# Unsplit fp32 operands in the first matmuls behind a normalisation: a two-layer decoder trunk on one core

## The chip, the cores and the metric

The kernel runs on one core of a Trainium2 chip. The metric is the device time of one execution in microseconds (us). The kernel before takes 1955.97 us, the median of three runs between 1953.8 and 1957.2.

## The reference

The reference is a decoder trunk of two layers on 256 tokens of width 1024, all in float32. Cut to what matters here:

```python
for l in range(2):
    h = rms_norm(x, norm1_g[l]) * (1.0 + sc1) + sh1
    z, xbc, dt_raw, mq, mk, mv, sq, sk, sv = split(h @ w_in[l])
    y = concat(ssd(z, xbc, dt_raw), moba(mq, mk, mv), swa(sq, sk, sv)) @ w_out[l]
    x = x + g1 * y
    h = rms_norm(x, norm2_g[l]) * (1.0 + sc2) + sh2
    q = h @ peer_wq[l]            # 8 heads x 256 columns
    # each half of q against 128 keys, top 16 of each, top 16 of the sums: 16 experts
    x = x + g2 * experts(h, chosen, peer_u[l], peer_v[l])
return rms_norm(x, final_g)
```

## The kernel before, in words

A product of two float32 matrices is made of three matmuls in the type fp32r (`mm3`, L165 to L168). Each operand is split into a high part (a cast to fp32r, on ScalarE: `wH` of weights at L159, `hH` of activations at L258) and a low part (what the cast left over: `wL` at L162, `hL` at L259), and high times high, high times low and low times high are added up in PSUM. The low part of a block of weights comes from VectorE (`low` is "v") or from GpSimd (as a whole, or as two halves where `low` is "h").

Weights come in blocks of 128 x 1024, four k-rows of 128 for 256 columns. `fetch` (L145) loads a block into one of five `raw` buffers by a DMA of the SP queue; `split` (L151) writes its parts into one of three `wH` and one of three `wL` buffers. A buffer is free for its next block when the last reader of the block in it is done. For `raw` that is the split.

`norm_rows`, `norm_scaled` and `norm_banks` make the scaled rows `xn` (L234) and transpose them on TensorE (L242). `norm_h` (L245) turns each of four transposed banks into `h32`, two k-rows of 256 tokens, one half on VectorE (L257) and one on ScalarE (L255), and then into `hH` and `hL`. There are two `norm_h` in a layer. The one ahead of the mixers goes in four steps of one bank (`FIRST`, L46): behind each step come the matmuls that need its two k-rows, for the column chunks `mq`, `mk` and `sq` in turn. The one behind the mixers does all four banks at once; behind it `peer` (L671) begins with `query(0)` (L713): 256 columns of `wq`, two blocks, `low` "h".

Most of the order on each engine is chosen by a planner that lists the instructions in advance by its own estimate of their times. Two things bind it: within `manual_schedule` (PE in `peer`, L711) the engine keeps the order of the program, and `pinned()` (L227) puts the instructions that its block issues on the engine of `pin[0]` behind `pin[0]`. `pin[0]` is the latest power operation of `norm_rows` on GpSimd (L222); so `query(0)`'s low parts on GpSimd come behind it.

Behind the eight queries and their scores (L725) come the passes over `peer_u` (L689) and `peer_v` (L899), in the same three-matmul form.

Of the kernel before, what the change touches and what calls it, by code (L numbers as in the profile page):

```python
# [13 lines left out]
F32 = mybir.dt.float32  # L14
# [3 lines left out]
ALU = mybir.AluOpType  # L18
# [4 lines left out]
P = 128  # L23
D = 1024
S = 256
NC = 2
KD = D // P
# [27 lines left out]
HB = 3  # L55
# [12 lines left out]
COLS = {"adab": 0, "n1": 48, "n2": 56, "cw": 64, "cb": 96, "mg": 104}  # L68
# [13 lines left out]
def trunk(ctx: ExitStack, tc: tile.TileContext, x_in, c_in, ada, cols, rows, w_in, w_out, wq, keysT, uT, vT, fg, out, dbg=None):  # L82
    nc = tc.nc
    V, A, G, T = nc.vector, nc.scalar, nc.gpsimd, nc.tensor
# [3 lines left out]
    st = ctx.enter_context(tc.tile_pool(name="st", bufs=2))  # L88
# [6 lines left out]
    def bank(kind=None):  # L95
        if kind is None:
            turn[0] += 1
            kind = "pa" if turn[0] % 2 else "pb" if turn[0] % 4 < 2 else "pc"
        return (ps_a if kind == "pa" else ps_b).tile([P, 512], F32, tag=kind, name=kind)
# [35 lines left out]
    hs = [None, None]  # L135
# [9 lines left out]
    def fetch(src):  # L145
        n = src.shape[-1]
        raw = st.tile([P, D + 1], F32, tag="raw", name="raw", bufs=RB)
        nc.sync.dma_start(raw[:, :n], src)
        return raw[:, :n]
# [15 lines left out]
    def mm3(o, l, r, start, stop):  # L165
        T.matmul(o, l[0], r[0], start=start, stop=False)  # L166
        T.matmul(o, l[0], r[1], start=False, stop=False)  # L167
        T.matmul(o, l[1], r[0], start=False, stop=stop)  # L168
# [44 lines left out]
    def norm_rows(pool, xt, c):  # L213
# [8 lines left out]
        pin[0] = G.tensor_tensor(out=r, in0=ms, in1=mhalf, op=ALU.pow).ins  # L222
        return r

    pin = [None]

    def pinned():  # L227

        return tc.issue_after(pin[0]) if PIN else nullcontext()
# [7 lines left out]
    def norm_banks(xn, k20=0, n=KD // 2, kind=None):  # L237
        banks = [bank(kind) for _ in range(n)]
        for c in range(NC):
            for k in range(2 * k20, 2 * (k20 + n)):  # L240
                o = k % 2 * S + c * P
                T.transpose(banks[k // 2 - k20][:, o:o + P], xn[c][:, k * P:(k + 1) * P], ident)  # L242
        return banks

    def norm_h(pool, banks, colt, modc, gcol, sh, sc, k20=0):  # L245
        k0, n = 2 * k20, 2 * len(banks)
        acol = pool.tile([P, KD], F32, tag="acol", name="acol")
        V.scalar_tensor_tensor(out=acol[:, k0:k0 + n], in0=modc[:, sc, k0:k0 + n], scalar=1.0, in1=colt[:, gcol + k0:gcol + k0 + n], op0=ALU.add, op1=ALU.mult)
        for k2 in range(k20, k20 + len(banks)):
            h32 = pool.tile([P, 2, S], F32, tag="t2k", name="h32", bufs=3)  # L250
            for q in range(2):
                k = 2 * k2 + q
                src = banks[k2 - k20][:, q * S:(q + 1) * S]
                if q and H32A:
                    A.activation(h32[:, q, :], src, AF.Identity, scale=acol[:, k:k + 1], bias=modc[:, sh, k:k + 1])  # L255
                else:
                    V.tensor_scalar(out=h32[:, q, :], in0=src, scalar1=acol[:, k:k + 1], scalar2=modc[:, sh, k:k + 1], op0=ALU.mult, op1=ALU.add)  # L257
            A.copy(hs[0][:, 2 * k2:2 * k2 + 2, :], h32)  # L258
            V.tensor_tensor(out=hs[1][:, 2 * k2:2 * k2 + 2, :], in0=h32, in1=hs[0][:, 2 * k2:2 * k2 + 2, :].bitcast(F32), op=ALU.subtract)  # L259

    def gated_add(pool, xt, c, n, acc, gb):

# [29 lines left out]
    def proj_channels(src, off, w, low=LOWM):  # L292

        pcs = [bank() for _ in range(w // P)]
        for _ in proj_parts(pcs, src, off, w, KD, low):
            pass
        return pcs

    def proj_parts(pcs, src, off, w, step, low=LOWM):

        for k0, n, h, lo in units(src, off, w, low):
            yield
            for k1 in range(0, n, step):
                for cb, pc in enumerate(pcs):
                    for kk in range(k1, min(n, k1 + step)):
                        k = k0 + kk
                        sl = slice(kk * w + cb * P, kk * w + (cb + 1) * P)
                        mm3(pc[:, :S], (h[:, sl], lo[:, sl]), (hs[0][:, k, :], hs[1][:, k, :]), k == 0, k == KD - 1)
                yield

    def proj_tokens(src, off, w, low=LOWM):
# [12 lines left out]
    def mixers(l, xp, mx, xt, xn, modc, colt, early, late):  # L324
        if True:
# [53 lines left out]
            off = {}  # L379
# [4 lines left out]
            wl = w_in[l]  # L384
# [99 lines left out]

            first = {n: [bank(b) for b in kinds] for n, kinds in (("mq", ("pa", "pa")), ("mk", ("pa", "pa")), ("sq", ("pb", "pb")))}
            part = {n: proj_parts(pcs, wl, *off[n], 2) for n, pcs in first.items()}
            for p, names in enumerate(FIRST):
                banks = norm_banks(xn, p, 1, "pc")
                pre, post = names
                pre = pre.split()  # L490
                ada = early(mx, 2 * p, 2)
                for i in range(max(len(pre), len(ada))):
                    if i < len(ada):
                        ada[i]()
                    if i < len(pre) and pre[i] != "-":
                        with pinned() if p == 1 else nullcontext():
                            next(part[pre[i]])
                norm_h(xp, banks, colt, modc, COLS["n1"], 0, 1, p)
                for n in post.split():
                    next(part[n])  # L500
            for g in part.values():
                assert next(g, None) is None
            tick[0] = later
            mq = to_sb(first["mq"], "mq")
            mk = to_sb(first["mk"], "mk")
            sq = to_sb(first["sq"], "sq")
            half = lambda t, i: t[64 * i:64 * (i + 1), :]
# [127 lines left out]
            pcs = [[bank() for _ in range(NC)] for _ in range(2)]  # L635
# [9 lines left out]
            for n in range(2):  # L645
                for q in range(2):
                    h, lo = split(fetch(w_out[l, n, 1, :, q * 1024:(q + 1) * 1024]), LOWM(q))
# [10 lines left out]
            xn = []  # L658
# [5 lines left out]
            for c in range(NC):  # L664
                for n in range(2):
                    gated_add(xp, xt, c, n, pcs[n][c], gb)
                xn.append(norm_scaled(xp, xt, c, norm_rows(xp, xt, c)))
            norm_h(xp, norm_banks(xn), colt, modc, COLS["n2"], 3, 4)


    def peer(l, steps):  # L671
# [23 lines left out]
        with tc.tile_pool(name=f"topk{l}", bufs=1, reuse_waits="tile") as tp:  # L695
# [15 lines left out]
            order.enter_context(tc.manual_schedule(engines={mybir.EngineType.PE}))  # L711

            def query(h):  # L713
                with pinned() if h == 0 else nullcontext():
                    pq = proj_channels(wq[l], h * D * 256, 256, lambda q: "h")
                q = new([P, 2, S], "q", bufs=2)
                for i in range(2):
                    A.copy(q[:, i, :], pq[i][:, :S])
                return q
# [204 lines left out]
    xp = xs.enter_context(tc.tile_pool(name="x0", bufs=1))  # L924
# [4 lines left out]
    xn = [norm_scaled(xp, xt, c, norm_rows(xp, xt, c)) for c in range(NC)]  # L929
    for l in range(DEPTH):  # L930
        ada0 = {}

        def early(pool, k0, n):
            if l:
                return []
            if not ada0:
                ada0.update({m: ada_steps(0, m, mod[0], pool) for m in range(2)})
            return [ada0[m][k] for k in range(k0, k0 + n) for m in range(2)]
# [24 lines left out]
        xp = xs.enter_context(tc.tile_pool(name=f"x{l + 1}", bufs=1, reuse_waits="tile"))  # L963
# [24 lines left out]
        else:  # L988
            xn = [norm_scaled(xp, xt, c, rs[c]) for c in range(NC)]
# [64 lines left out]
```

## Time and profile before

| | |
|---|---|
| median of three runs | 1955.97 us |
| the profiled execution | 1956.04 us, of which the span from the first to the last instruction is 1954.3 us |
| PE (TensorE) busy | 1875.9 us, 96% of the span |
| DVE (VectorE) busy | 1430.5 us, 73% |
| ACT (ScalarE) busy | 966.3 us, 49% |
| POOL (GpSimd) busy | 498.1 us, 25% |
| DMA | 376.53 MB, 193 GB/s in the mean |

The span is 1.7 us shorter than the execution's time. Times in the rows below are counted from the start of the span. The busy time of PE counts matmuls that overlap once; a matmul's own duration is longer than the distance from its start to the next one's. The granted clock is given as a share of 2.4 GHz, so 0.50 is 1.2 GHz. PEld is the weight load.

### The profile page before, as it was taken

What the parts mean: (1) busy time and instruction counts of PE and PEld (TensorE: products, weight loads), DVE (VectorE), ACT (ScalarE), POOL (GpSimd) and SP (SyncE); (2) the same over time, 40 slices, a digit from 0 to 9 for tenths busy, and PEclk for the clock granted to TensorE, in tenths of its full rate; (3) what the DMA queues carried; (4) which work ended last, traced back from release to release, by engine and by line L of the source; (5) the groups of instructions that cost most, each with busy time, mean ns of one, the idle gap of its engine ahead of it and who ended that gap; (6) DMA issues with size and microseconds to landing.
All of it is one profiled execution on the core that took longest, in us unless ns stands there. A gap on an engine that the chain in (4) does not pass through costs nothing. (4 is left out here: it accounts for less than half of the span.)

```text
span 1954.3 us, 33671 instructions
## 1 busy us (share of the span) xinstructions
PE 1875.9 (96%) x12864; PEld 1714.5 (88%) x12864; DVE 1430.5 (73%) x2679; ACT 966.3 (49%) x1502; POOL 498.1 (25%) x303
## 2 busy tenths in 40 slices
PE   4898999999999999999989989999999999999998
PEld 3786999999999888888878789999999998888886
DVE  6866799889963898966667669968899346666665
ACT  3464445444444454545547444455444445555544
POOL 5675799100024001000001167960000320000001
PEclk8898999999999999999989989999999999999999
DMA  7863455444455999866543344554444555655553
GB/s 276 288 211 116 162 182 182 167 162 153 161 166 172 380 348 350 312 199 195 192 131 123 118 143 150 186 178 159 160 155 160 173 193 190 223 196 193 193 194 116
DMA packets 103557, 376.53 MB, mean 193 GB/s; under 512 B 12002, under 2 KB 12258, under 8 KB 102756
## 3 DMA queue, kind: packets, MB, share of 16 engines
q1 hardware_dynamic: 103396, 374.39, 56.3%
q8 instruction: 100, 1.64, 0.3%
q14 instruction: 61, 0.50, 0.1%
HBM read 371.20 MB, written 3.15 MB: 192 GB/s over the span
## 5 line engine op out<-in xcount | busy, mean ns | idle before, releaser
L159 ACT CAST wH<-raw 128x1024 fp32r<-128x1024 f32 (+1 forms) x602 | 629.3, 1046 | 530.7 <-PE pu L167 349.9
L162 DVE TENSOR_TENSOR wL<-raw,wH 128x1024 fp32r<-128x1024 f32 x437 | 535.3, 1226 | 223.6 <-ACT wH L159 222.8
L162 POOL TENSOR_TENSOR wL<-raw,wH 128x512 fp32r<-128x512 f32 (+2 forms) x224 | 438.4, 1977 | 595.7 <-ACT wH L159 586.0
L166 PE MATMUL pu<-hH,wH 128*128 128x256 f32 x2048 | 581.2, 284 | 3.9 <-ACT act L693 3.9
L168 PE MATMUL pu<-hH,wL 128*128 128x256 f32 x2048 | 575.7, 281 | 0.0
L167 PE MATMUL pu<-hL,wH 128*128 128x256 f32 x2048 | 575.4, 281 | 0.0
L167 PE MATMUL pacc<-wL,aH 128*128 128x512 f32 x1024 | 399.2, 390 | 0.0
L168 PE MATMUL pacc<-wH,aL 128*128 128x512 f32 x1024 | 398.5, 389 | 0.0
L166 PEld LDWEIGHTS pu<-hH,wH 128*128 128x128 f32 x2048 | 386.9, 189 | 4.6 <-ACT act L693 4.6
L167 PEld LDWEIGHTS pu<-hL,wH 128*128 128x128 f32 x2048 | 387.1, 189 | 0.0
L168 PEld LDWEIGHTS pu<-hH,wL 128*128 128x128 f32 x2048 | 386.5, 189 | 0.0
L166 PE MATMUL pacc<-wH,aH 128*128 128x512 f32 x1024 | 277.4, 389 | 0.0
L892 ACT CAST aH<-act 128x256 fp32r<-128x256 f32 x256 | 104.0, 408 | 340.3 <-PE pacc L167 339.0
L167 PEld LDWEIGHTS pacc<-wL,aH 128*128 128x128 f32 x1024 | 192.2, 188 | 40.4 <-DVE wL L162 0.8
L168 PEld LDWEIGHTS pacc<-wH,aL 128*128 128x128 f32 x1024 | 192.2, 188 | 39.7
L166 PEld LDWEIGHTS pacc<-wH,aH 128*128 128x128 f32 x1024 | 192.1, 188 | 39.8
L893 DVE TENSOR_TENSOR aL<-act,aH 128x256 fp32r<-128x256 f32 x256 | 108.4, 425 | 108.6 <-ACT aH L892 108.2
L980 POOL TENSOR_TENSOR x<-x,fgb 128x512 f32<-128x512 f32 x2 | 3.4, 1700 | 352.4 <-ACT junk L218 352.4
L166 PE MATMUL pa<-hH,wH 128*128 128x256 f32 x256 | 75.7, 308 | 12.5 <-ACT hH L258 8.7
L167 PE MATMUL pa<-hL,wH 128*128 128x256 f32 x256 | 76.4, 301 | 1.9 <-DVE hL L259 1.8
L168 PE MATMUL pa<-hH,wL 128*128 128x256 f32 x256 | 75.6, 299 | 0.9 <-POOL wL L162 0.9
L854 DVE SCALAR_TENSOR_TENSOR act<-pc,act 128x160 f32<-128x160 f32 (+30 forms) x126 | 38.5, 306 | 44.5 <-PE pc L848 44.3
(428 smaller groups left out, 2470.9 us busy)
## 6 DMA issues: line engine op xcount, KB each, us to landing
raw<-in_uT_dram SPq DMA_DIRECT2D x256, 512.0 KB, 3.6
raw<-in_vT_dram SPq DMA_DIRECT2D x256, 512.0 KB, 4.4
adaw<-in_ada_dram SPq DMA_DIRECT2D x56, 512.5 KB, 5.9
raw<-in_ada_dram SPq DMA_DIRECT2D x40, 512.5 KB, 4.9
raw<-in_w_in_dram SPq DMA_DIRECT2D x38, 512.0 KB, 4.8
raw<-in_wq_dram SPq DMA_DIRECT2D x32, 512.0 KB, 3.6
raw<-in_w_out_dram SPq DMA_DIRECT2D x16, 512.0 KB, 3.9
raw<-in_w_in_dram SPq DMA_DIRECT2D x8, 392.0 KB, 3.5
```

The source lines that it names most:

```text
L159: A.copy(h[:, :n], src)
L162: eng.tensor_tensor(out=lo[:, o:o + step], in0=src[:, o:o + step], in1=h[:, o:o + step].bitcast(F32), op=ALU.subtract)
L166: T.matmul(o, l[0], r[0], start=start, stop=False)
L167: T.matmul(o, l[0], r[1], start=False, stop=False)
L168: T.matmul(o, l[1], r[0], start=False, stop=stop)
L854: V.scalar_tensor_tensor(out=a, in0=pv[:, lo:hi, :], scalar=1.0 / WSCALE, in1=a, op0=ALU.mult, op1=ALU.mult)
L892: A.copy(aH, act)
L893: V.tensor_tensor(out=aL, in0=act, in1=aH.bitcast(F32), op=ALU.subtract)
L980: (V if c else G).tensor_tensor(out=xt[:, c, cs], in0=xt[:, c, cs], in1=fgb[:, cs], op=ALU.mult)
```

## The change

For layer 1's chunk `mq`, and for `query(0)` of both layers, the three matmuls on split operands become one matmul on the float32 operands as they are: `raw` as loaded and `h32` as computed, in the new `proj_parts_whole`. These blocks are not split. `h32` is kept: where `norm_h` does all four banks, it stands in two buffers of the ring `wL` (four k-rows in each); where it does one bank, in the ring `t2k` as before. The making of `hH` and `hL` is put into functions that are called behind the matmuls on `h32` instead of ahead of them. `pin[0]` becomes the last `h32` instruction on VectorE in the `norm_h` of four banks; `query(0)` is no longer pinned, `query(1)` is, and its low parts move from GpSimd to VectorE. Layer 0's first `norm_h` and its chunks stay as they are.

```diff
-    def norm_h(pool, banks, colt, modc, gcol, sh, sc, k20=0):
+    def norm_h(pool, banks, colt, modc, gcol, sh, sc, k20=0, whole=None):
...
+        halves = []
         for k2 in range(k20, k20 + len(banks)):
-            h32 = pool.tile([P, 2, S], F32, tag="t2k", name="h32", bufs=3)
+            if whole is None or k20 or len(banks) == 1:
+                h32 = pool.tile([P, 2, S], F32, tag="t2k", name="h32", bufs=3)
+            elif k2 % 2 == 0:
+                four = st.tile([P, 1024], F32, tag="wL", name="h32", bufs=HB).rearrange("p (k t) -> p k t", k=4)
+                h32 = four[:, 0:2, :]
+            else:
+                h32 = four[:, 2:4, :]
+            if whole is not None:
+                whole.append(h32)
...
+                    d = V.tensor_scalar(out=h32[:, q, :], in0=src, scalar1=acol[:, k:k + 1], scalar2=modc[:, sh, k:k + 1], op0=ALU.mult, op1=ALU.add)
+                    if whole is not None and len(banks) > 1:
+                        pin[0] = d.ins
+
+            def half(k2=k2, h32=h32):
+                A.copy(hs[0][:, 2 * k2:2 * k2 + 2, :], h32)
+                V.tensor_tensor(out=hs[1][:, 2 * k2:2 * k2 + 2, :], in0=h32, in1=hs[0][:, 2 * k2:2 * k2 + 2, :].bitcast(F32), op=ALU.subtract)
+            if whole is None:
+                half()
+            else:
+                halves.append(half)
+        return halves
...
+    def proj_parts_whole(pcs, src, off, w, step, hw):
+
+        ku = 1024 // w
+        blk = src[off:off + KD * P * w].rearrange("(r p q f) -> r p q f", p=P, r=KD // min(KD, 2 * ku), f=ku * w)
+        for k0 in range(0, KD, ku):
+            raw = fetch(blk[k0 // (2 * ku), :, k0 // ku % 2, :])
+            yield
+            for k1 in range(0, ku, step):
+                for cb, pc in enumerate(pcs):
+                    for kk in range(k1, k1 + step):
+                        k = k0 + kk
+                        T.matmul(pc[:, :S], raw[:, kk * w + cb * P:kk * w + (cb + 1) * P], hw[k // 2][:, k % 2, :], start=k == 0, stop=k == KD - 1)
                 yield
...
+            whole = None
+            if l:
+                whole = []
+                part["mq"] = proj_parts_whole(first["mq"], wl, *off["mq"], 2, whole)
...
-                norm_h(xp, banks, colt, modc, COLS["n1"], 0, 1, p)
+                halves = norm_h(xp, banks, colt, modc, COLS["n1"], 0, 1, p, whole)
                 for n in post.split():
                     next(part[n])
+                    if n == "mq":
+                        for f in halves:
+                            f()
...
-            norm_h(xp, norm_banks(xn), colt, modc, COLS["n2"], 3, 4)
+            whole2[:] = []
+            whole2_halves[:] = norm_h(xp, norm_banks(xn), colt, modc, COLS["n2"], 3, 4, 0, whole2)
...
             def query(h):
-                with pinned() if h == 0 else nullcontext():
-                    pq = proj_channels(wq[l], h * D * 256, 256, lambda q: "h")
+                if h == 0:
+
+                    pq = [bank() for _ in range(2)]
+                    for _ in proj_parts_whole(pq, wq[l], 0, 256, 4, whole2):
+                        pass
+                    for f in whole2_halves:
+                        f()
+                else:
+                    with pinned() if h == 1 else nullcontext():
+                        pq = proj_channels(wq[l], h * D * 256, 256, lambda q: "v" if h == 1 else "h")
```

## Rows read from the trace of the kernel before

**Rows 1.** The table of stretches: the stretch and its length, then busy time and number of instructions of PE, PEld, DVE, ACT and POOL, the granted clock, the DMA engines' mean busy share and GB/s.

```profile
175.00:200.00 25.00, 19.39 (x116) 17.02 (x114) 13.09 (x19) 11.88 (x23) 16.01 (x13) 0.80 0.38 133
200.00:300.00 100.00, 100.00 (x855) 100.00 (x854) 91.75 (x408) 49.04 (x65) 85.04 (x45) 1.00 0.52 174
...
600.00:1010.00 410.00, 403.67 (x1962) 341.08 (x1961) 296.58 (x407) 204.23 (x299) 24.61 (x22) 0.99 0.73 259
...
1130.00:1160.00 30.00, 25.35 (x177) 23.73 (x177) 15.20 (x46) 12.95 (x22) 22.58 (x18) 0.83 0.46 160
```

**Rows 2.** The timeline of all engines at the end of layer 0's mixers: start, duration (of the whole group where it is x2 or more), engine, line, operation, out<-in, and the idle time ahead of it with what ended it.

```profile
179.22 0.89 DVE L234 TENSOR_SCALAR xn<-x,hr 128x512 f32<-128x512 f32 x2 [0.44 <-POOL hr L222]
...
179.76 0.44 PE L242 MATMUL pa<-ident,xn 128*128 128x128 f32 x2 [2.51 <-DVE xn L234]
...
180.47 0.38 PE L242 MATMUL pc<-ident,xn 128*128 128x128 f32 x2
180.82 8.68 POOL L162 TENSOR_TENSOR wL<-raw,wH 128x512 fp32r<-128x512 f32 x6
180.89 2.88 DVE L234 TENSOR_SCALAR xn<-x,hr 128x512 f32<-128x512 f32 x2 [0.66 <-POOL hr L222]
...
182.42 0.69 PE L242 MATMUL pa<-ident,xn 128*128 128x128 f32 x2 [1.56 <-DVE xn L234]
...
183.69 0.53 DVE L257 TENSOR_SCALAR h<-pa,acol,modc 128x256 f32<-128x256 f32 x1
...
184.32 0.56 ACT L255 ACTIVATE h<-pa,modc,acol 128x256 f32<-128x256 f32 x1 [4.73 <-DVE h L257]
...
185.24 0.61 ACT L258 CAST hH<-h 128x512 fp32r<-128x512 f32 x1
...
185.88 0.79 DVE L259 TENSOR_TENSOR hL<-h,hH 128x512 fp32r<-128x512 f32 x1 [0.75 <-ACT hH L258]
...
185.90 0.58 PE L166 MATMUL pa<-hH,wH 128*128 128x256 f32 x1 [0.96 <-ACT hH L258]
...
188.41 0.58 PE L167 MATMUL pa<-hL,wH 128*128 128x256 f32 x1
```

**Rows 3.** The timeline of PE alone, on through layer 0's query 0 (its last matmul is the one ahead of 195.08) and to the scores behind query 1.

```profile
191.78 0.41 PE L167 MATMUL pb<-hL,wH 128*128 128x256 f32 x1
...
192.20 0.28 PE L166 MATMUL pa<-hH,wH 128*128 128x256 f32 x1
192.32 0.28 PE L167 MATMUL pa<-hL,wH 128*128 128x256 f32 x1
...
194.96 0.28 PE L168 MATMUL pb<-hH,wL 128*128 128x256 f32 x1
195.08 0.28 PE L166 MATMUL pa<-hH,wH 128*128 128x256 f32 x1
...
200.84 1.05 PE L725 MATMUL pa<-kt,q 128*128 128x128 f32 x8
201.65 0.36 PE L166 MATMUL pb<-hH,wH 128*128 128x256 f32 x1
```

**Rows 4.** The table of stretches again, columns as in rows 1, for short stretches around the three places where the clock falls and rises.

```profile
182.00:186.00 4.00, 2.33 (x9) 1.53 (x9) 3.25 (x6) 1.68 (x4) 4.00 (x4) 0.50 0.34 98
...
192.00:193.00 1.00, 1.00 (x9) 1.00 (x9) 0.00 (x0) 0.72 (x1) 0.00 (x0) 0.91 0.13 49
...
1144.00:1145.00 1.00, 1.00 (x8) 1.00 (x8) 0.00 (x0) 0.98 (x1) 0.00 (x0) 0.75 0.00 0
...
1004.00:1005.00 1.00, 1.00 (x8) 1.00 (x7) 0.00 (x0) 0.00 (x0) 0.00 (x0) 0.72 0.00 0
```

**Rows 5.** The timeline of all engines at the end of layer 1's mixers, columns as in rows 2; the last of them is the first matmul of query 1.

```profile
1132.64 2.88 DVE L234 TENSOR_SCALAR xn<-x,hr 128x512 f32<-128x512 f32 x2 [0.66 <-POOL hr L222]
...
1137.65 0.58 PE L166 MATMUL pa<-hH,wH 128*128 128x256 f32 x1 [0.96 <-ACT hH L258]
...
1147.03 0.28 PE L166 MATMUL pa<-hH,wH 128*128 128x256 f32 x1
```

**Rows 6.** The timeline of PE in layer 1's mixers: two matmuls of float32 operands, 256 columns each, of which each is recorded as two instructions; then, of the view of that line, all eight such instructions (shortest, median and longest in ns).

```profile
1089.27 1.03 PE L594 MATMUL pa<-one,bmt 128*128 128x256 f32 x4
...
L594 PE MATMUL pa<-one,bmt x8: 377/379/381, 140.3 to 1089.9; 128*128 128x256 f32 x8
```

**Rows 7.** From the page: the group of the casts that make wH (count, busy us and mean ns of one, idle time ahead of them), and the loads of wq (count, KB of each, median us from issue to landing).

```profile
L159 ACT CAST wH<-raw 128x1024 fp32r<-128x1024 f32 (+1 forms) x602 | 629.3, 1046 | 530.7 <-PE pu L167 349.9
...
raw<-in_wq_dram SPq DMA_DIRECT2D x32, 512.0 KB, 3.6
```

**Rows 8.** The timeline of all engines at the start of layer 1, columns as in rows 2.

```profile
992.46 1.22 DVE L162 TENSOR_TENSOR wL<-raw,wH 128x1024 fp32r<-128x1024 f32 x1
...
994.32 1.22 DVE L162 TENSOR_TENSOR wL<-raw,wH 128x1024 fp32r<-128x1024 f32 x1
...
998.29 0.54 DVE L257 TENSOR_SCALAR h<-pc,acol,modc 128x256 f32<-128x256 f32 x1 [0.39 <-PE pc L242]
998.93 0.57 ACT L255 ACTIVATE h<-pc,modc,acol 128x256 f32<-128x256 f32 x1 [3.02 <-DVE h L257]
999.52 0.62 ACT L258 CAST hH<-h 128x512 fp32r<-128x512 f32 x1
...
1000.31 1.20 PE L166 MATMUL pa<-hH,wH 128*128 128x256 f32 x4
```

More of the change, by code (lines that the diff above doesn't have):

```diff
@@ L223, in norm_rows @@
         return r
+    whole2, whole2_halves = [], []
     pin = [None]
@@ L256, in norm_h @@
                 else:
-                    V.tensor_scalar(out=h32[:, q, :], in0=src, scalar1=acol[:, k:k + 1], scalar2=modc[:, sh, k:k + 1], op0=ALU.mult, op1=ALU.add)
-            A.copy(hs[0][:, 2 * k2:2 * k2 + 2, :], h32)
-            V.tensor_tensor(out=hs[1][:, 2 * k2:2 * k2 + 2, :], in0=h32, in1=hs[0][:, 2 * k2:2 * k2 + 2, :].bitcast(F32), op=ALU.subtract)
+                    d = V.tensor_scalar(out=h32[:, q, :], in0=src, scalar1=acol[:, k:k + 1], scalar2=modc[:, sh, k:k + 1], op0=ALU.mult, op1=ALU.add)
[9 more added lines that the diff above has]
+        return halves
     def gated_add(pool, xt, c, n, acc, gb):
@@ L308, in proj_parts @@
                         mm3(pc[:, :S], (h[:, sl], lo[:, sl]), (hs[0][:, k, :], hs[1][:, k, :]), k == 0, k == KD - 1)
+                yield
[4 more added lines that the diff above has]
+            raw = fetch(blk[k0 // (2 * ku), :, k0 // ku % 2, :])
+            yield
+            for k1 in range(0, ku, step):
[3 more added lines that the diff above has]
+                        T.matmul(pc[:, :S], raw[:, kk * w + cb * P:kk * w + (cb + 1) * P], hw[k // 2][:, k % 2, :], start=k == 0, stop=k == KD - 1)
                 yield
```

## The prediction

> **What bounds the kernel now.** I read the table of stretches first. Behind the starts of the two expert stages PE is busy all the time (100.00 of 100.00 us) at the full clock, while DVE and POOL are busy for 92 and 85; through 600 to 1010, 403.67 of 410 [rows 1]. So the end of the kernel is set by PE's work plus the few places where PE waits or runs at the low clock, and a microsecond gained at such a place reaches the end, as long as nothing behind it becomes late. The places that the change touches are the starts of the two expert stages (175 to 200: PE busy 19.39 of 25 at a mean clock of 0.80; 1130 to 1160: 25.35 of 30 at 0.83) [rows 1] and the start of layer 1.
>
> The timeline then shows the chain at 180 us [rows 2]. The scaled rows `xn` of the first 128 tokens take 0.89 us for two pieces on DVE, those of the second 128 take 2.88. The difference is that POOL began its six low parts (8.68 us) at 180.82, just ahead of them: the low parts of `query(0)`, which were tied behind POOL's power operation. Then come the transposes, `h32` on DVE (0.53) and ACT (0.56), the cast to `hH` (0.61), the first matmul at 185.90, `hL` (0.79), a second wait, and a third one before 188.41. PE runs at the low clock from before 182.42 until the rise: the stretch 192 to 193 has a mean of 0.91, so the rise is at 192.2 [rows 4]. Query 0 ends at 195.08, where query 1 begins [rows 3]. In layer 1 it is the same picture 951.75 us later: `xn` 2.88 us at 1132.64, first matmul at 1137.65, query 1 from 1147.03 [rows 5].
>
> **Step 1, the start of query 0 (gain 2.9 us).** No low part of query 0 is made any more, and those of query 1 go to DVE behind `h32`, so POOL has nothing to do here: the first block that still goes to it is query 2's, and its buffer in the `wL` ring is held by `h32` until query 0 is nearly done. So I take 0.445 us for each piece of `xn`, as for the first tokens: ready at 181.34 and 181.78 instead of 182.33 and 183.77. The eight transposes behind them start some 0.1 us later as they did at 179.76, and last 1 us at the pace of 179.76 to 180.85, 2 us at the low clock [rows 2]: done near 183.0. `h32` of the first bank is on DVE from about 182.2: k-row 0 is ready at 182.75, ACT's k-row 1 at 183.3; the other banks follow at 0.55 us. The cast and `hL` (0.61 and 0.79) are no longer ahead of the matmuls. First matmul: 183.0 instead of 185.90. In the rows the matmul at 185.90 went as soon as the first of four casts into the one tile `hH` was done, so a reader waits for its part alone; if here it waited for all four writes of a buffer, that is 183.9. I take 183.0, and 1134.75 in layer 1.
>
> **Step 2, query 0's own length (costs back a part).** 48 fp32r matmuls become 16 of float32. An fp32r matmul goes every 0.21 us at the low clock and every 0.12 at the full one (191.78 to 192.20, 192.20 to 192.32) [rows 3]. A float32 matmul of 256 columns is two instructions; four instructions last 1.03 us, and one 0.379, so they follow at (1.03 - 0.38) / 3 = 0.217 and a matmul takes 0.433 us at the full clock [rows 6]. The scores give a little less: eight instructions of 128 columns in 201.65 - 200.84 = 0.81 us, or 0.405 us for 256 columns [rows 3]. No row shows this form at the low clock: between 0.433 (if the clock did not matter) and twice that, 0.866. fp32r went from 0.12 to 0.21, so I take 0.866. At the full clock a query costs 16 x 0.433 = 6.9 us instead of 48 x 0.12 = 5.8.
>
> The clock rose 6.3 us behind the first matmul in layer 0 (192.2 - 185.9), 6.8 in layer 1 (1144.5 - 1137.65), both with waits of up to half a microsecond in between, and 4.25 at the start of layer 1 (1004.56 - 1000.31), where matmuls followed more closely [rows 2, 4, 5, 8]. Here nothing interrupts them, so I take 5.0. Then 5.0 / 0.866 = 5.8 matmuls are done at the low clock, and the other 10.2 take 4.4: 9.4 us in all. Query 0 ends at 192.4 instead of 195.08 and at 1144.15 instead of 1147.03: **2.7 and 2.9 us earlier**. With 4.25 it is 9.05 us, with 6.8 it is 10.35; with a price that ignores the clock, 6.9.
>
> **Step 3, what moves behind it (nothing).** Query 1 now needs at 192.4: `hH` (four casts, 0.61 each, on ACT behind `h32`'s end at 184.9: 187.4), `hL` (four of 0.79 on DVE, until about 188.2 [rows 2]), and its own split: a cast of 1.05 [rows 7] and 1.22 on DVE [rows 8], the first block's done before 190.7 even if it comes last. Its second block's `wL` needs the first `h32` buffer back, after eight matmuls: 183.0 + 5.0 + 2.2 x 0.433 = 188.95, and is wanted at 192.4 + 24 x 0.12 = 195.3. Query 2's first block on POOL starts at 192.4 with the second buffer back, takes two halves (8.68 / 6 = 1.45 each), and is wanted at 198.2. On SP's queue the load of query 2's second block now waits for PE's reading of `raw`, until 188.95, and not for a split; 3.6 us to landing [rows 7], a cast and POOL's 2.9 make 196.5, wanted at 201. So all lies beside PE's work. If the planner puts `hL` or `wL` later on DVE, PE waits at query 1 for what is missing.
>
> **Step 4, the start of layer 1 (cost 0.5).** `mq` costs 6.9 - 5.8 = 1.2 us more at the full clock. Its first matmuls go when `h32` is there (998.9 to 999.5) and not at 1000.31 behind `hH`: up to 1.4 us of work at the low clock, worth 0.7 at the full one. The two splits between `xn`'s inputs on DVE (992.46 and 994.32, 1.22 each [rows 8]) belong to `mk` and `sq`; `mq`'s block is no longer split, so one could go, but the `wH` buffer that it leaves goes to `mk`'s second block, and I expect the planner to put that there. Net +0.5; bounds: -0.7 if one split leaves the chain, +1.9 if the first matmul is not earlier and meets the low clock. `mq`'s first `raw` is held until PE has read it, near 1003, and the load behind it on SP's queue, `sq`'s second block, waits for that: 3.6 us to landing, a cast of 1.05 and 1.22 on DVE make 1009. It is wanted in the last of the stage's six blocks, some 120 x 0.12 = 14 us behind 1000.31, so that costs nothing.
>
> **Sum.** 1956.04 (the profiled execution; 0.07 above the median) - 2.7 - 2.9 + 0.5 = **1950.9 us**.
>
> **Rivals.**
> *The clock rises sooner.* The transposes behind `xn` now run into the matmuls without a gap, so PE is at work from about 181.4 and not from 183.0. If they counted, the rise would come 3.4 us behind the first matmul: 3.9 matmuls low, 12.1 x 0.433 = 5.2, in all 8.6 us; 0.8 less for each query: 1949.3. For it: the gap of 0.8 us ahead of 185.90 is gone. Against it: from 182 to 186 PE was busy 2.33 of 4 us, mostly with transposes, and the clock stayed at 0.50 [rows 4]. If a rise fell still earlier, or the clock did not fall at all (6.9 us a query), it would be down to 1946.
> The Trainium skill, TensorE: Matmul & The Clock Gate, section Part 4: PE-mode transpose, says that transposes do not count as work for the clock as matmuls do. By that rule the rise is counted from 183.0, which is the forecast, and this rival falls; the trace's stretch agrees but cannot tell work too thin from work of the wrong kind.
>
> *The gain is used up behind the start.* DVE now carries `hL` and two `wL` of 1.22 within some 6 us, and a planned order can put them behind one another badly; or `h32` is waited for as a whole (0.9 us each), or the planner finds other work for ACT or POOL in the chain of `xn` (a cast of 1.05 us [rows 7] ahead of the sum of squares). 1 to 2 us in each layer: 1953 to 1955. For it: PE's next need comes earlier than before. Against it: the margins of step 3, 1.7 us and more.
>
> *The clock stays low through query 0 (slower).* Should PE at float32 not bring the clock up, 16 x 0.866 = 13.9 us: query 0 ends at 196.9 and 1148.65, 1.8 and 1.6 later than before, and `mq` adds the upper bound of 1.9: 1961.3. It decides where the rise comes later than 10.3 us behind the first matmul: 10.3 + (16 - 10.3 / 0.866) x 0.433 = 12.1, what there is from 183.0 to 195.08. For it: no stretch of dense float32 matmuls at the low clock is in the rows. Against it: all three rises came within 6.8 us [rows 4], with thinner work.
>
> **How the numbers follow.** The forecast (its own range 1949 to 1953, from rises of 4.25 to 6.8 and step 4's bounds) has a chance of 0.58, the sooner clock 0.12, the gain used up 0.22, the low clock 0.08. The range reaches into the second and third: 1947.5 to 1955.5. What a measurement tells from no change is 0.2%, 3.9 us: under 1952.1 is faster, over 1959.9 slower. The sooner clock and most of the forecast (0.48 of 0.58) are faster: 0.60; the rest of it and the used-up gain make 0.32; slower 0.08.
>
> **What would show it.** Right: `xn` of the second tokens in about 0.9 us with POOL idle; first float32 matmul near 183.0 and 1134.8, no wait of PE up to query 1, and query 1's first matmul near 192.4 and 1144.2; layer 1's start within a microsecond of before. Wrong: a wait of PE for `hL` or `wL` at query 1; matmuls of 0.866 us up to its end; `xn` still at 2.9 us; or a shift in layer 1's mixers of more than 2 us, for which I have no term.

## The result, and the profile after

The changed kernel takes **1943.67 us** (median of five runs, 1939.51 to 1946.02); the kernel before, beside it, 1954.68 (1953.8 to 1957.2). The ratio is 0.9939, interval 0.9923 to 0.9955. Two later measurements of the same kernel gave 1943.49 and 1942.72. The forecast was 1950.9, with a range of 1947.5 to 1955.5: the sign was right, and the gain, some 11 us, is twice the 5.1 that was worked out. The profiled execution took 1944.28 us, its span 1942.6.

The first place to look is the same stretch in both kernels: 25 us from the last matmul of the output projections on (the last `pa<-oH,yL`, 176.85 and 1128.61 before; 174.75 and 1120.44 after). The table of stretches of the kernel after, columns as in [rows 1]; first the two starts, then short stretches around the rises of the clock there, and last one at the start of layer 1:

```profile
174.75:199.75 25.00, 21.92 (x144) 20.08 (x143) 13.37 (x42) 10.68 (x22) 9.42 (x9) 0.93 0.52 179
1120.44:1145.44 25.00, 21.92 (x143) 20.12 (x142) 13.31 (x42) 10.68 (x22) 9.37 (x9) 0.93 0.53 179
...
180.00:183.00 3.00, 3.00 (x10) 2.55 (x9) 3.00 (x6) 2.62 (x6) 0.00 (x0) 0.50 0.03 5
183.00:184.00 1.00, 1.00 (x5) 0.83 (x5) 1.00 (x3) 1.00 (x3) 0.00 (x0) 0.86 0.18 33
...
1128.00:1129.00 1.00, 1.00 (x4) 0.79 (x4) 1.00 (x2) 1.00 (x4) 0.00 (x0) 0.62 0.00 0
...
995.00:996.00 1.00, 1.00 (x5) 0.86 (x4) 0.75 (x2) 0.94 (x2) 0.00 (x0) 0.68 0.00 0
```

PE is busy for 21.92 us of such a stretch, and its mean clock is 0.93. The kernel before, profiled once more (e1 below), has 19.39 us and 0.80 in it. So two things differ, not one: PE waits 2.5 us less, and it runs faster. A mean of 0.86 between 183 and 184 puts the rise at 183.3, 2.7 us behind the first matmul of query 0; 0.62 between 1128 and 1129 puts it at 1128.8, 2.3 us behind. Before, it was 6.3 and 6.8 us [rows 4]. In the three later profiles with an unsplit query 0 and an idle GpSimd (e2, e4 and e11 below) it is 1.1 to 2.6 us, and at one start of e4 the clock does not fall at all.

The timeline of the kernel after at the end of layer 0's mixers, which answers to [rows 2, 3] (xn is now L235, `h32` L267 and L265, the casts L272, the low halves L273, the unsplit matmuls L341):

```profile
178.20 0.55 POOL L222 TENSOR_TENSOR hr<-hm,mhalf 128x1 f32<-128x1 f32 x1 [1.12 <-DVE hm L220]
...
178.78 0.88 DVE L235 TENSOR_SCALAR xn<-x,hr 128x512 f32<-128x512 f32 x2 [0.66 <-POOL hr L222]
179.32 0.44 PE L243 MATMUL pa<-ident,xn 128*128 128x128 f32 x2 [0.57 <-DVE xn L235]
...
179.80 0.54 DVE L267 TENSOR_SCALAR h<-pa,acol,modc 128x256 f32<-128x256 f32 x1
...
180.61 3.21 PE L341 MATMUL pa<-h,raw 128*128 128x256 f32 x8
...
180.84 0.56 ACT L265 ACTIVATE h<-pb,modc,acol 128x256 f32<-128x256 f32 x1
...
181.61 1.22 DVE L162 TENSOR_TENSOR wL<-raw,wH 128x1024 fp32r<-128x1024 f32 x1
...
182.74 2.50 DVE L273 TENSOR_TENSOR hL<-h,hH 128x512 fp32r<-128x512 f32 x4
...
183.66 1.89 PE L341 MATMUL pb<-h,raw 128*128 128x256 f32 x8
185.38 1.89 PE L341 MATMUL pa<-h,raw 128*128 128x256 f32 x8
...
187.11 1.89 PE L341 MATMUL pb<-h,raw 128*128 128x256 f32 x8
...
188.65 0.47 PE L166 MATMUL pa<-hH,wH 128*128 128x256 f32 x1
...
189.08 1.29 POOL L162 TENSOR_TENSOR wL<-raw,wH 128x512 fp32r<-128x512 f32 x1 [10.34 <-PE pb L341]
```

POOL does nothing between 178.75 and 189.08, and the second `xn` takes 0.88 us where it took 2.88. Behind 179.32 no row of PE has idle time in brackets, up to query 1 and beyond. Query 0 lasts 188.65 - 180.61 = 8.04 us (9.18 before); the 32 instructions of its 16 matmuls come at (185.38 - 183.66) / 8 = 0.215 us each at the full clock. Layer 1 is alike, with 7.85 us:

```profile
1124.47 0.88 DVE L235 TENSOR_SCALAR xn<-x,hr 128x512 f32<-128x512 f32 x2 [0.66 <-POOL hr L222]
...
1126.49 3.02 PE L341 MATMUL pa<-h,raw 128*128 128x256 f32 x8
...
1134.34 0.47 PE L166 MATMUL pa<-hH,wH 128*128 128x256 f32 x1
```

The start of layer 1, which answers to [rows 8]: the two splits of 1.22 us are still in DVE's chain ahead of `xn`, and `mq`'s first matmul follows the transposes without a cast between them.

```profile
987.12 1.22 DVE L162 TENSOR_TENSOR wL<-raw,wH 128x1024 fp32r<-128x1024 f32 x1
...
988.98 1.22 DVE L162 TENSOR_TENSOR wL<-raw,wH 128x1024 fp32r<-128x1024 f32 x1
...
991.26 2.07 PE L243 MATMUL pc<-ident,xn 128*128 128x128 f32 x8 [5.46 <-DVE xn L235]
993.54 3.02 PE L341 MATMUL pa<-h,raw 128*128 128x256 f32 x8 [0.21 <-DVE h L267]
```

For the experiments I take three times from each kernel's timeline of PE: the last matmul of the output projections, query 0's first matmul, and the first matmul of the scores (`kt,q`), by which queries 0 and 1 are done. "Start" is the first distance, "queries" the second. Before: 9.05 and 14.94 us in layer 0, 9.04 and 15.00 in layer 1. After: 5.86 and 13.86, 6.05 and 13.73. Start and queries together are 24.0 us twice before, 19.7 and 19.8 after: **8.5 us of the gain are there**. At the start of layer 1, from the last matmul of layer 0's experts to the first one of the attention, it is 29.2 before and 28.5 after.

### The profile page after: what moved, and what is told of

It is laid out like the page before. It is cut to its first block, busy times and chain, and to the rows that moved or that the text cites. A ratio compares the mean times of both kernels' runs of the same rounds, so it can differ in the third digit from the quotient of the medians.

```text
span 1942.6 us, 33542 instructions
## 1 busy us (share of the span) xinstructions
PE 1870.3 (96%) x12816; PEld 1708.6 (88%) x12816; DVE 1423.6 (73%) x2681; ACT 959.9 (49%) x1496; POOL 473.9 (24%) x287
## 5 line engine op out<-in xcount | busy, mean ns | idle before, releaser
L159 ACT CAST wH<-raw 128x1024 fp32r<-128x1024 f32 x596 | 622.9, 1046 | 522.8 <-PE pu L167 352.7
L162 POOL TENSOR_TENSOR wL<-raw,wH 128x1024 fp32r<-128x1024 f32 (+2 forms) x208 | 414.7, 2012 | 611.2 <-ACT wH L159 585.5
L166 PE MATMUL pa<-hH,wH 128*128 128x256 f32 x224 | 66.2, 306 | 10.6 <-ACT hH L272 7.6
L178 DVE SCALAR_TENSOR_TENSOR raw<-raw,crow 128x1025 f32<-128x1025 f32 x40 | 61.9, 1558 | 11.1 <-DMA raw<-in_ada_dram 9.0
L178 DVE SCALAR_TENSOR_TENSOR adaw<-adaw,crow 128x1025 f32<-128x1025 f32 x56 | 68.3, 1226 | 1.2 <-ACT crow L130 1.2
```

The source lines that it names most:

```text
L159: A.copy(h[:, :n], src)
L162: eng.tensor_tensor(out=lo[:, o:o + step], in0=src[:, o:o + step], in1=h[:, o:o + step].bitcast(F32), op=ALU.subtract)
L178: V.scalar_tensor_tensor(out=src, in0=src, scalar=1.0, in1=cond, op0=ALU.mult, op1=ALU.mult, accum_out=modc[:, m, k:k + 1])
```

## The experiments

Theory A: the gain is made at the starts, by an earlier first matmul and by a clock that rises sooner behind it. Beside each group of runs the kernel before was timed on the same chip; its medians were 1954.6 to 1955.4.

**e1 and e4: both kernels once more, as they are.** In their profiles the mixers of layer 0 and the rest of layer 1's mixers had differed by 2 us each, without a change there.

> The kernel before, unchanged, in a second profiled execution. Theory A (what the traces of before and after differ by in the mixers is not the change's): about 1954 to 1957 us, but the mixers' ends move by 1 to 4 us against the first profile (177.2 us for layer 0, and 132 us from layer 1's first transposes to the end of its output projection), because the two short stretches at the low clock (160 to 180 at a mean of 0.91, 1100 to 1110 at 0.83) lie elsewhere or are missing. Theory B (the change also gains in the mixers): both ends within 0.5 us of the first profile, with the same two low stretches.

> The changed kernel again. Both theories: 1939 to 1946 us, as in its first five runs. In its second profile, by theory A the starts of query 1 stay 11.4 to 11.8 us behind the last matmul of the output projections (13.5 and 13.9), while the mixers' ends move with the low stretches; by theory B the mixers' ends stay.

e1: 1955.08, ratio 1.0 (0.9988 to 1.0013). e4: 1943.49, ratio 0.995 (0.9933 to 0.9967). e1's start and queries are 9.05 and 14.95, 9.05 and 14.58 us; e4's 6.33 and 13.07, 5.65 and 12.81. Query 1 starts 13.9 us behind the last matmul of the output projections in both layers of the first profile after (the 11.4 to 11.8 of the expectation is not in the rows), and 13.6 and 12.6 us in e4. The stretches of e1's two starts:

```profile
175.54:200.54 25.00, 19.39 (x123) 17.38 (x122) 11.37 (x17) 10.80 (x21) 17.73 (x14) 0.80 0.43 152
1125.05:1150.05 25.00, 19.39 (x126) 17.37 (x125) 11.38 (x17) 11.16 (x22) 17.77 (x15) 0.80 0.44 152
```

Layer 1's mixers behind the first attention matmul take 108.6 us in the first profile of before, 106.4 in e1, 106.5 after: that difference belongs to the execution, not to the change. The first profile of before has a short stretch at the low clock there, and the other two have none:

```profile
1103.50:1107.00 3.50, 3.50 (x10) 2.72 (x10) 0.00 (x0) 0.69 (x1) 3.11 (x3) 0.51 0.00 0
```

The starts repeat within a few tenths for the kernel before; after, they vary by a microsecond, as the clock does (mean 0.93 in three of these four starts, 1.00 in e4's second).

**e2 and e3: each half of the change alone.** e2 leaves `mq` split, e3 leaves query 0 split.

```diff
-            if l:
+            if False:
                 whole = []
```

> Unsplit operands in query 0 of both layers, layer 1's chunk mq as before. Theory A (the two starts make the gain): 8.8 us at the two queries, less about 2 us in the expert passes: 1945 to 1949, ratio near 0.996. Theory B (layer 1's start and mixers make 2.8 of it): the gain of e4 less 2.8 us.

> Unsplit operands in layer 1's chunk mq alone, query 0 as before. Theory A: 0.7 us at the start of layer 1 and nothing elsewhere: within 2 us of before, ratio 0.999 to 1.000. Theory B: 2 to 3 us faster, ratio near 0.9985.

e2: 1944.65, ratio 0.995 (0.9933 to 0.9966). e3 (`query`, and the call of `norm_h` ahead of it, as in the kernel before): 1952.76, ratio 0.9988 (0.9976 to 1.0001). Most of the gain comes with query 0; e2 lies at the lower edge of A's range. The start of layer 1 takes 28.4 us in e3 and 29.4 in e2. Over all profiles without spare matmuls there, it is 28.2 to 29.0 us with an unsplit `mq` (five profiles, mean 28.5) and 28.6 to 29.4 with a split one (six, mean 29.0): a gain of some 0.5 us, and not a loss. e3's time is 2.3 us below the kernel before by its ratio, which is nearer to B's figure than to A's and more than its profile shows. Its interval reaches from 4.7 us faster to no change, so what `mq` is worth in the time stays open.

**e5: GpSimd held back, operands still split.** The low parts of query 0 wait for the second `xn`:

```diff
-            norm_h(xp, norm_banks(xn), colt, modc, COLS["n2"], 3, 4)
+            banks2 = norm_banks(xn)
+            hold = xp.tile([P, 1], F32, tag="hold", name="hold")
+            pin[0] = G.tensor_tensor(out=hold, in0=xn[1][:, D - 1:D], in1=mhalf, op=ALU.mult).ins
+            norm_h(xp, banks2, colt, modc, COLS["n2"], 3, 4)
```

> The kernel before, its split operands kept, but query 0's low parts on GpSimd begin only behind the second xn (one small GpSimd operation that reads that xn stands ahead of them). Theory A, the gain of the change lies in an earlier first matmul (a second xn without GpSimd beside it) and in an earlier rise of the clock behind it: the second xn takes about 0.9 us in place of 2.88, the first matmul comes 1.5 to 2 us earlier at each start, and the time is 2 to 5 us below the kernel before (1950.5 to 1953.5), the rest of the change's 11 being the clock's. Theory B, the gain comes from the missing split alone (no cast, no low parts ahead of the first matmul): the second xn is short here too, but the low parts come late by as much and the query waits for them; time as before within 1 us (1954.4 to 1956.4).

1951.41, ratio 0.9982 (0.9972 to 0.9992): inside A's range. The start is 7.5 us in both layers, 1.5 shorter, but the queries take 15.0 and 15.7 us. The timeline of layer 1 shows what comes instead, and two lines of the table of stretches stand behind it:

```profile
1129.43 9.30 POOL L162 TENSOR_TENSOR wL<-raw,wH 128x512 fp32r<-128x512 f32 x6
...
1131.85 0.39 PE L166 MATMUL pa<-hH,wH 128*128 128x256 f32 x1 [1.30 <-ACT hH L258]
...
1132.57 0.38 PE L167 MATMUL pa<-hL,wH 128*128 128x256 f32 x1 [0.34 <-DVE hL L259]
...
1132.79 0.28 PE L168 MATMUL pa<-hH,wL 128*128 128x256 f32 x1
1132.92 0.28 PE L166 MATMUL pa<-hH,wH 128*128 128x256 f32 x1
...
1133.09 4.50 DVE L259 TENSOR_TENSOR hL<-h,hH 128x512 fp32r<-128x512 f32 x3
...
1134.27 0.58 PE L167 MATMUL pa<-hL,wH 128*128 128x256 f32 x1 [0.71 <-DVE hL L259]
1134.64 0.42 PE L168 MATMUL pa<-hH,wL 128*128 128x256 f32 x1
...
1140.38 0.28 PE L168 MATMUL pa<-hH,wL 128*128 128x256 f32 x1
...
1131.00:1133.50 2.50, 1.31 (x7) 0.95 (x7) 1.64 (x4) 2.50 (x6) 2.50 (x2) 1.00 0.19 52
1133.00:1134.00 1.00, 0.55 (x5) 0.34 (x3) 1.00 (x2) 0.97 (x3) 1.00 (x2) 0.75 0.89 246
```

The disturbance has moved from `xn` to `hL`: three of them take 4.50 us beside POOL (2.50 for four in the kernel after, where POOL is idle). Query 0 begins at the full clock here (0.13 us from matmul to matmul at 1132.79), behind a wait of 1.30 us for the cast. It waits 0.34 and 0.71 us for `hL`, and from 1134.27 on its matmuls follow at 0.21 us until 1140.3. The mean of 0.75 between 1133 and 1134 puts the fall of the clock at 1133.5. There the wait of 0.71 us begins: the fall comes behind 2.5 us in which PE was busy for 1.31, and that last wait lies in the low stretch already. So a query that starts at the full clock can lose it again among such waits; what one wait alone costs isn't shown.

**e6: unsplit operands, GpSimd busy.** Query 1's low parts go to POOL again, tied behind the power operation:

```diff
-                    if whole is not None and len(banks) > 1:
-                        pin[0] = d.ins
...
-                        pq = proj_channels(wq[l], h * D * 256, 256, lambda q: "v" if h == 1 else "h")
+                        pq = proj_channels(wq[l], h * D * 256, 256, lambda q: "h")
```

> The changed kernel, query 0 unsplit, but GpSimd is given work beside the second xn again: it makes low parts of query 1 there, in place of VectorE behind h. Theory A: xn takes 2.88 us again, the first matmul comes 2 us later at each start, and the time is 3 to 6 us above the changed kernel (1946.5 to 1949.5), more if the rise of the clock slips as well. Theory B: the first matmul waits for neither cast nor low parts, so the time stays within 1 us of the changed kernel (1942.7 to 1944.7). It also tells whether the 1.1 us by which the expert pass is longer in every kernel with an unsplit query 0 (398.8 us against 397.7 from the first matmul of its first sum to the first of its second) hangs on who writes query 1's low parts: 397.7 here if it does, 398.8 if it doesn't.

1947.67, ratio 0.9963 (0.9949 to 0.9977): A. The second `xn` is back at its old length, the start at 7.9 us twice, and the queries take 14.1 and 14.55:

```profile
180.30 2.68 POOL L162 TENSOR_TENSOR wL<-raw,wH 128x512 fp32r<-128x512 f32 x2
180.36 2.89 DVE L235 TENSOR_SCALAR xn<-x,hr 128x512 f32<-128x512 f32 x2 [0.66 <-POOL hr L222]
...
184.22 3.44 PE L339 MATMUL pa<-h,raw 128*128 128x256 f32 x8
```

So of the 3.1 us by which the start shortened (9.05 to about 5.95 in the first profile), 1.9 are the undisturbed `xn` and 1.15 the cast that no longer stands ahead of the first matmul. In the time, the held GpSimd alone (e5) gave 3.7 us and the unsplit operands beside a busy GpSimd (e6, with `mq`) 7.5; the changed kernel gave 11 to 12, about the sum of the two. The side question is answered too: the expert pass (layer 0, as in the expectation) took 399.0 us here, but 398.8 in e5, whose operands are split, and 397.7 in e12 below, whose query is unsplit. The microsecond does not hang on the change.

**e7, e8 and e9: the clock kept up by spare matmuls.** Their sums are overwritten. In e7 and e8 they stand around the transposes, in the kernel before and in the changed one (e8 has eleven more ahead of layer 1's first transposes); e9 is e5 with those of e7.

```diff
-    def norm_banks(xn, k20=0, n=KD // 2, kind=None):
+    def norm_banks(xn, k20=0, n=KD // 2, kind=None, warm=None):
         banks = [bank(kind) for _ in range(n)]
+        if warm is not None:
+            for _ in range(5):
+                T.matmul(banks[-1][:, :S], ident, warm, start=True, stop=True)
         for c in range(NC):
+            if warm is not None and c:
+                for o in (P, S + P):
+                    T.matmul(banks[-1][:, o:o + P], ident, xn[0][:, :P], start=True, stop=True)
```

> The kernel before with spare float32 matmuls (five of 256 columns ahead of the transposes of h in each layer, two of 128 columns between the two token chunks; their sums are overwritten and are no part of the result), which keep TensorE busy where it otherwise waits for the normalisation. Theory A: if the clock of query 0 is what those waits set, the granted clock is 1 within a few us of the first matmul in place of 6.3 us behind it, query 0's 48 matmuls run at 0.12 us each for most of their length (5.8 us all at full clock against 9.2), and the time is 2 to 6 us below the kernel before (1949.5 to 1953.5). Theory B: the clock isn't what bounds query 0's length (its low parts are), and the time is that of the kernel before within 1 us or slightly worse for the added work.

> The changed kernel with the same spare matmuls, and eleven more ahead of the first transposes of layer 1 (all overwritten, no part of the result). Theory A: query 0's 16 matmuls run at 0.433 us (6.9 us in place of 8.0 and 7.9), layer 1's first chunk of columns at full clock too, and the time is 2 to 4 us below the changed kernel (1939.5 to 1942). Theory B: the spare matmuls hold the transposes up or do nothing for the clock: 1943.5 to 1946.

> The kernel before, all operands split, with both the held GpSimd operation and the spare matmuls (overwritten, no part of the result). Theory A, what the change gained is the undisturbed second xn and the clock, and the unsplit operands are only the way to them: no or next to no low clock at either start, first matmul some 7 us behind the last matmul of the output projections (9.05 before, 5.86 after), query 0's 48 matmuls in about 6 us, first scores some 19 to 20.5 us behind that matmul (24.0 before, 19.7 after), and the time is 7 to 10 us below the kernel before (1945 to 1948). Theory B, the missing split itself carries most of it: the low parts (GpSimd needed 9.25 us for six in the kernel with the held operation) hold query 0 up whatever the clock, first scores at 22 us or more, and the time is less than 5 us below the kernel before (1950 to 1955).

e7: 1953.2, ratio 0.9997 (0.9986 to 1.0008): no gain that the interval shows, so B by the time. The first matmul still waits 1.42 us for the cast behind the disturbed `xn`, and layer 0's query runs at the low clock for its first 6 us all the same; start 9.05 us as before, queries 14.7 and 13.8. e9: 1950.93, ratio 0.999 (0.9979 to 1.0001), its profiled execution 1944.36. Its start is 7.3 us, near the 7 expected, its queries 14.1 and 14.15, together 21.4 us: between A's 20.5 and B's 22, and in the time with B. Its waits, from the timeline of PE in layer 0, and a line of its table of stretches:

```profile
179.88 0.39 PE L166 MATMUL pa<-hH,wH 128*128 128x256 f32 x1 [1.60 <-ACT hH L264]
180.85 0.39 PE L167 MATMUL pa<-hL,wH 128*128 128x256 f32 x1 [0.58 <-DVE hL L265]
...
182.54 0.58 PE L167 MATMUL pa<-hL,wH 128*128 128x256 f32 x1 [0.28 <-DVE hL L265]
...
181.00:182.00 1.00, 1.00 (x6) 0.97 (x6) 1.00 (x2) 0.84 (x2) 1.00 (x2) 0.58 0.60 147
```

A matmul behind a wait lasts 0.39 us in the first two rows and 0.58 in the third: the query begins at the full clock and falls to the low one at 181.2 (mean of 0.58 between 181 and 182), behind the waits for the cast and the first low half and ahead of the third wait. B's cause, `wL` that comes late, is not seen: no wait in that stretch names `wL`. What holds split operands back is the cast and `hL` ahead of the first matmuls. The unsplit ones have neither, and that is why they, and not a quieter GpSimd alone, bring most of the gain.

e8: 1942.53, ratio 0.9943 (0.9929 to 0.9958), between the ranges of A and B; its profiled execution 1938.42. Start and queries are 5.64 and 12.88 us, and 5.65 and 12.87.

**e11 and e12: the changed kernel and e8, side by side.**

> The changed kernel a third time, unchanged, beside the two others of this call: 1942 to 1946 by both theories. For the comparison with the one with spare matmuls on the same chip, and for a third reading of the low clock at the two starts (so far one short stretch in three of four starts, none in the fourth).

> The changed kernel with spare matmuls, a second time. If the clock's last part is worth what the two starts show (18.3 us from the last output projection to the first scores in place of 19.7, twice, and about 1 us at the start of layer 1), it is 2 to 4 us below the changed kernel of the same call; if those were readings of one execution, within 1 us of it.

e11: 1942.72, ratio 0.9941 (0.9928 to 0.9955). e12: 1942.89, ratio 0.9942 (0.9928 to 0.9956). The stretches of e12's two starts:

```profile
176.38:201.38 25.00, 24.52 (x168) 22.38 (x167) 14.55 (x51) 11.02 (x23) 10.63 (x10) 1.00 0.56 195
1123.67:1148.67 25.00, 24.52 (x168) 22.38 (x167) 14.49 (x51) 11.03 (x23) 10.63 (x10) 1.00 0.57 195
```

The clock never falls at the two starts (12.81 and 12.87 us for the queries, which is their length at the full clock), and the start of layer 1 takes 27.2 us where e11 has 28.2. With start and queries (18.5 twice in place of 19.7 and 19.8; the 18.3 of the expectation is counted from the first spare matmul, 0.23 us later) that is 3.6 us in the profile, and e12's time is that of e11. The gain at the starts is no chance of one execution, as e8's profile has the same 18.5 twice. But in e12's profile layer 1's mixers take 110.1 us behind the first attention matmul where e11 has 106.4. The table of stretches shows what differs, two short stretches at the low clock in those mixers:

```profile
1044.00:1048.00 4.00, 3.96 (x17) 3.56 (x17) 3.80 (x10) 3.04 (x4) 0.55 (x1) 0.57 0.40 131
1098.50:1102.50 4.00, 4.00 (x13) 3.17 (x13) 0.26 (x1) 1.04 (x1) 3.15 (x3) 0.57 0.00 0
```

In the seven profiles that have none there, these mixers take 106.3 to 106.5 us, and in the five with one 107.6 to 108.7. Such a stretch comes and goes in one and the same kernel (before has it, e1 does not), but all four profiles with spare matmuls have one or two, and of the nine others only two have one. Whether spare matmuls bring them about stays open, and there is no version here that beats the changed kernel measurably.

Start and queries, from one profile of each form (us; layer 0, layer 1; mean clock of the 25 us; time):

| kernel | start | queries | clock | time |
|---|---|---|---|---|
| before (e1) | 9.05, 9.05 | 14.95, 14.58 | 0.80, 0.80 | 1955.1 |
| e5, split, GpSimd held | 7.51, 7.55 | 14.98, 15.69 | 0.80, 0.80 | 1951.4 |
| e7, split, spare matmuls | 9.05, 9.04 | 14.73, 13.83 | 0.86, 0.93 | 1953.2 |
| e9, split, held and spare | 7.26, 7.27 | 14.12, 14.15 | 0.93, 0.93 | 1950.9 |
| e6, unsplit, GpSimd busy | 7.89, 7.88 | 14.10, 14.55 | 0.86, 0.86 | 1947.7 |
| after | 5.86, 6.05 | 13.86, 13.73 | 0.93, 0.93 | 1943.7 |
| e12, after with spare | 5.65, 5.65 | 12.81, 12.87 | 1.00, 1.00 | 1942.9 |

## Why the prediction was wrong, by its steps

**Step 1 was right.** It gave 2.9 us for the start, from an undisturbed `xn` and the cast behind; measured are 3.2 and 3.0 in the first profiles, and the mean of the eight starts with an unsplit query 0 and an idle GpSimd (the kernel after, e2, e4, e11) is 6.08 us, against 9.05: 2.97. A reader waits for its own part of a buffer, as assumed: the first matmul starts at 180.61, while ACT writes the same buffer until 181.40.

**Step 2 failed, in one term: "Here nothing interrupts them, so I take 5.0".** The prices beside it held: 0.433 us for a float32 matmul at the full clock (measured 2 x 0.215), twice that at the low one (the first eight instructions take 3.05 us, from 180.61 to 183.66; 2.7 us at 0.433 and 0.36 behind the rise at 0.215 make 6.2 + 1.7 = 7.9 of them). But the rise came 2.7 and 2.3 us behind the first matmul, and in e6 about 3.1 and 3.9. A low microsecond gives half the work, so 2.5 us less of them make the query (5.0 - 2.5) / 2 = 1.25 us shorter: 9.4 - 1.25 = 8.15, and 8.04 and 7.85 were measured. Instead of a cost of 0.2 us in layer 0 and none in layer 1, query 0 brought a gain of 1.1 and 1.5. The three rises from which I took the number (4.25 to 6.8) all stood behind waits of PE; I had written that waits of up to half a microsecond lay in them, and still used them as ends of the range. A place without waits and without transposes lies elsewhere in the kernel before. In layer 1's experts PE waits 2.08 us and then runs split matmuls without a pause (timeline of PE, then the table of stretches):

```profile
1201.66 0.38 PE L166 MATMUL pu<-hH,wH 128*128 128x256 f32 x1 [2.08 <-ACT act L693]
...
1202.00:1203.00 1.00, 1.00 (x9) 1.00 (x8) 1.00 (x2) 0.09 (x1) 0.13 (x1) 0.76 0.25 98
1205.00:1206.00 1.00, 1.00 (x6) 1.00 (x6) 1.00 (x7) 0.00 (x0) 0.00 (x0) 0.53 0.03 12
```

The clock falls at 1202.5 and rises at 1205.9, 4.3 us behind that first matmul; in the seven profiles whose clock falls there, it is 3.3 to 4.6. In the six starts of before, e1 and e3, with waits among their matmuls, it is 5.2 to 6.8. So the waits explain only a part of the error, and a split matmul does not by itself keep the clock low for longer. The larger part is where I let the count begin. In the seven starts with an unsplit query 0 and an idle GpSimd at which the clock fell, the rise came 1.1 to 2.7 us behind the first matmul, but 2.8 to 4.0 behind the first of the second transposes, from which on PE has no wait. This is read from rows; no run changed the waits or the transposes alone.

That makes *the clock rises sooner* the rival that came true, and more than it said: it took a rise 3.4 us behind the first matmul and gave 1949.3, with 1946 as the far end. By the rule of the Trainium skill, TensorE: Matmul & The Clock Gate, section Part 4: PE-mode transpose, that transposes do not count as work for the clock as matmuls do, the rise would be counted from the first matmul on. The rows above speak against that here (1.1 to 2.7 us against 3.3 to 4.6), but no run had the transposes without matmuls behind them, so the rule itself is not refuted.

**Step 3 was right.** Behind the second transposes PE waits for nothing in either start; query 1 finds `hH`, `hL` and `wL` ready, and `wL` stood on DVE at 181.61, ahead of `hL`, as was allowed for. *The gain is used up behind the start* did not come.

**Step 4 had the wrong sign.** It expected both splits to stay in the chain, which they did, and the first matmul 1.4 us earlier, which it was (8.12 us behind the last expert matmul in place of 9.55). But it put +0.5 on it; e3 against e1 gives -0.8, and the mean of all profiles -0.5. Again it is the clock as far as the rows go: a mean of 0.68 between 995 and 996 puts the rise at 995.6, 2.1 us behind the first matmul, where it was 4.25 before [rows 4, 8]. It is 1.5 to 3.1 in the five profiles with an unsplit `mq` and 3.4 to 5.0 in the six with a split one.

**The sum.** Traced: 2 x 2.97 for the starts, 2 x (14.78 - 13.43) for the queries (means of the six of before, e1 and e3, and of the same eight), 0.5 for `mq`: 9.1 us. Timed: about 11.5. The other 2.4 us are not placed by these profiles; single executions of one kernel differ by as much in the mixers. The forecast's own range was also a little short: with a rise at 6.8 us and +1.9 for `mq`, its upper end is 1954.3 and not 1953.

Most of the traced gain is the clock's. PE waits 2.5 us less at each start, but an unsplit query costs 1.1 us more at the full clock, and `mq` 1.2 more once; the wait ahead of `mq` shrinks from 0.87 to 0.21 us. By these rows that leaves 2 x (2.5 - 1.1) - 1.2 + 0.7 = 2.3 us without the clock, an estimate. The whole runs agree: their mean granted clock was 0.9814 over 77 runs of the kernel before and 0.9875 over 19 of the one after. A straight line through the 77 gives 1.3 us less for 0.001 more clock, so 0.0061 goes with some 8 of the 11.5 us. At an equal clock of 0.986 the one run of the kernel before took 1949.5 us, and the four of the changed kernel 1945.3 in the mean.

*The clock stays low through query 0* fell: behind query 0's first float32 matmul the clock rose within 2.7 us in the changed kernel, and within 3.9 in e6.

## What to carry to other kernels

At a place where TensorE starts behind a chain of small operations, count its waits in the first microseconds as well as its work: the starts of the kernel before, with waits among their matmuls, ran at the low clock until 5.2 to 6.8 us behind the first one, those with an unsplit query 0 and no such waits until 1.1 to 3.9 or not at all. A form with more work for TensorE and fewer steps ahead of it (a float32 matmul of 0.43 us in place of three fp32r ones of 0.36) can be the faster one for that reason. Take the delay of a clock rise from a row with the same waits in it, and the same work of TensorE ahead of it, as the new code will have, or keep both ends in the range.

## What was not expected of the hardware

A GpSimd subtraction beside VectorE stretches some of VectorE's operations: `xn` (one float32 input of 128x512) from 0.44 to 1.44 us a piece, and `hL` from 0.63 to as much as 1.50 (the mean of three in e5; 0.79 for the first one before [rows 2]). It leaves others as they are: `h32`, which VectorE reads from PSUM, takes 0.53 us beside GpSimd at 183.69 [rows 2] and 0.54 without it at 179.80 after. Holding GpSimd back moved the loss from the one to the other.

Keeping the clock up by hand was worth 3.6 us in the profile at the starts (e12 against e11) and nothing that can be measured in the time: 1942.5 and 1942.9 against 1943.7, 1943.5 and 1942.7.
